# Layer norm shift as a TensorE product, own buffers for the modulation products, partition moves on GpSimd: one change to a two-layer encoder trunk

## Chip, core and metric

The kernel runs on one core of one Trainium2 chip. A core has TensorE (PE; PEld is its weight load), VectorE (DVE), ScalarE (ACT), GpSimd (POOL) and SyncE (SP, which here only issues DMAs). The metric is the device time of one execution in microseconds. Times before are a median of three runs; one more execution was profiled.

## The reference

Two layers on x of 512 tokens by 1024 features, float32. Layer 0 mixes tokens by windowed attention (8 query heads, 2 key/value heads, a sink per head), layer 1 by a recurrent block (a convolution of width 4 and a gated linear recurrence in both directions). A squared-ReLU MLP with 4096 hidden features follows each. Each of the four sub-layers is modulated by the condition `c` and ends in a layer norm:

```python
for i in range(DEPTH):                     # 2 layers, two sub-layers each
    shift, scale, gate = split(silu(c) @ ada_w[i, 0] + ada_b[i, 0], 3)
    h = x * (1.0 + scale) + shift
    y = windowed_gqa(h, ...) if i % 2 == 0 else recurrent_block(h, ...)
    x = layer_norm(ALPHA * x + (1.0 + gate) * y, ln_g[i, 0], ln_b[i, 0])
    shift, scale, gate = split(silu(c) @ ada_w[i, 1] + ada_b[i, 1], 3)
    y = square(relu((x * (1.0 + scale) + shift) @ mlp_w1[i])) @ mlp_w2[i]
    x = layer_norm(ALPHA * x + (1.0 + gate) * y, ln_g[i, 1], ln_b[i, 1])
```

So the norm of one sub-layer and the modulation of the next are one affine step: with n the normalised x, h = n · g(1 + scale) + (b(1 + scale) + shift).

## The kernel before

**Instructions and order.** Python code adds operations to a list with a priority (`Program.add`), a planner (`schedule`) gives each a modelled cost, simulates the five engines and emits them in the order of the simulated starts. So a changed cost, buffer or priority changes the order on every engine. Each engine, and each DMA queue (SP's, POOL's), works in that order. All instructions are emitted at one line, 483; the profile's groups are told apart by tile names.

**Products.** A float32 matrix is split into a rounded high part and a remainder, and a product is three TensorE passes (`mm3`). Weights come in units of 128 x 1024 floats (512 KB): SP loads one into one of four `raw` slots, ScalarE writes the high part into one of six `w` slots, VectorE subtracts for the low part (`conv_unit`). `keep_raw` holds slots back from the weights. Activations lie transposed in `ht` (8192 columns: high, then low), hidden ones in `hid`.

**Modulation.** A row of 1024 (a shift, scale or gate) is a gemv, `gemv_tasks`: eight 512 KB pieces of `ada_w` are loaded, each into a `raw` slot, and VectorE multiplies each by a column of silu(c) and adds into an accumulator. Then the partitions are summed, by TensorE with a matrix of ones in the attention part and by GpSimd's all-reduce in the first MLP. The tasks wait in a list; `bg` takes some after each head (`BH`), each value tile (`BV`) or each tile group of the MLP (`RATE`). Rows for later are kept in DRAM (`mods`). `mod_rows` folds norm and modulation: `rows[3]` becomes g(1 + scale) and `rows[4]` the shift b(1 + scale) + shift, each on all 128 partitions.

**Layer norm.** `last_sink` evacuates an output tile of 128 tokens (`evac`: gate, residual add, statistics) and `ln_block` finishes it. For each half of 512 features ScalarE normalises, VectorE multiplies by `rows[3]` into `u` and adds `rows[4]` into `h`, TensorE transposes `h` in four 128 x 128 blocks into a PSUM bank, and ScalarE and VectorE split the bank into `ht`. The next products need it. Three norms do this, four tiles of two halves each; the last norm writes the output instead. Then VectorE and an accumulating DMA of GpSimd (`xb<-rows`) make the residual.

**Moves between partitions.** Partial rotary embedding (`rope`) packs 32 rows of up to four heads, rotates them together and moves them back (10 moves). In the recurrent block 128-wide tiles hold blocks of 96 channels and a third of a fourth block: `conv` moves 32 rows of the high and low part (6 per group of tiles, four groups), `gates` moves 9 sigmoid outputs and 4 collected tiles per group. All 86 are DMAs on SP's queue. GpSimd's queue has 9 accumulating DMAs of the recurrence (`w<-w`, `ex<-ex`) and 12 of the norms.

Of the kernel before, what the change touches and what calls it, by code (L numbers as in the profile page):

```python
# [14 lines left out]
D = 1024  # L15
# [55 lines left out]
def pack(inp):  # L71
# [91 lines left out]
    out["ident"] = np.eye(128, dtype=np.float32)  # L163
    return out
# [13 lines left out]
class View:  # L178
# [20 lines left out]

    def partition_broadcast(self, n):  # L200
        return View(self.tile, self.p0, self.p1, self.cols, self.ops + (("pb", n),))
# [11 lines left out]
    def get(self):  # L213
        v = self.tile.real[:, :]
        for op in self.ops:
            if op[0] == "i":
                v = v[op[1]]
            elif op[0] == "r":
                v = v.rearrange(op[1], **op[2])
            elif op[0] == "pb":  # L220
# [13 lines left out]
class Program:  # L234
# [60 lines left out]
    def price(self, op, reads, writes):  # L295
        n = 1
        w = writes[0] if writes else reads[0]
        for d in w.shape[1:]:
            n *= d
        op.table, op.nbytes = 0, 0  # L300
        ps = any(v.tile.kind == "ps" for v in reads)
        aps = sum(isinstance(op.kw.get(k), View) for k in ("scalar1", "scalar2", "scalar", "bias", "scale", "accum_out"))
        if op.eng == "tensor":
            passes = 1 if op.fn == "transpose" or op.kw["rhs"].ops[-1][0] == "b" else 4
            op.nbytes = passes * n * (reads[0].p1 - reads[0].p0) / 128
            op.cost = 109 if op.fn == "transpose" else max(107 if passes == 1 else 213, passes * n * 0.4167 + 16)
        elif op.eng == "scalar":
            op.cost = n * 0.833 + (51 if ps else 94) + 93 * aps
            op.table = TABLES.get(op.kw["func"].name, 0) if "func" in op.kw else 0
        elif op.eng == "vector":  # L310
            if op.fn == "bn_stats":
                op.cost = reads[0].shape[1] * 1.042 + 68
            elif op.fn in ("tensor_scalar", "tensor_copy") and not ps:
                op.cost = n * 0.52 + 69 + 60 * aps
            elif op.fn == "tensor_tensor_scan":
                op.cost = n * 2.083 + 65
            else:
                op.cost = n * 1.042 + 65 + (60 if aps else 0)
        elif op.eng == "gpsimd" and op.fn == "dma_start":
            op.cost = 1000  # L320
        elif op.eng == "gpsimd":
            op.cost = {"memset": n * 0.85, "tensor_scalar": n * 3.4 + 105, "partition_all_reduce": n * 7.0}.get(op.fn, n * 2.105 + 147)
        else:
            p = w.shape[0]
            op.nbytes = p * n * 4
            op.cost = 600
        op.end = op.start = None

        n_in = sum(v.tile.kind == "sb" and v.shape[-1] > 0 for k, v in op.kw.items() if isinstance(v, View) and k in ("in0", "in1", "in_", "data0", "data1"))
        if op.eng == "vector":  # L330
            two = n_in == 2 or op.fn in ("tensor_scalar", "tensor_copy") and not ps and writes[0].tile.kind == "sb" and n % 2 == 0
            op.lock = two
        else:
            op.lock = op.eng == "gpsimd" and op.fn not in ("memset", "dma_start")

    def schedule(self):
# [36 lines left out]
        while len(order) < total:  # L373
# [101 lines left out]
    def emit(self, nc, tc, pools):  # L475
        fix = lambda a: self.real(a, pools)
        with tc.manual_schedule():
            order = self.schedule()
            self.place(order, pools)
            for op in order:  # L480
                args = [fix(a) for a in op.args]
                kw = {k: fix(a) for k, a in op.kw.items()}
                op.ins = getattr(getattr(nc, op.eng), op.fn)(*args, **kw)  # L483
# [3 lines left out]
        [128, "ht", "rows", "acc2"]  # L487
        + [f"ex{i}" for i in range(17) if i not in (12, 13)]
# [5 lines left out]
        + [f"hid{i}" for i in range(16)]  # L494
# [36 lines left out]
class Kernel:  # L531
    def __init__(self, I, O):
# [6 lines left out]
        self.ht = t("ht", 8192)  # L539
        self.hid = [t(f"hid{i}", 512) for i in range(16)]  # L540
        self.xb = [t(f"xb{i}", 1024) for i in range(TB)]
        self.rx = t("rows", 6144)
        self.rows = [self.rx[:, 1024 * i : 1024 * i + 1024] for i in range(5)]
        self.ex = [t(f"ex{i}", 512) if i not in (12, 13) else self.rx[:, 512 * i - 1024 : 512 * i - 512] for i in range(17)]
        self.ident = t("ident", 128)
# [12 lines left out]


    def renew(self, kind, idx):  # L560
        n = {"hid": 512, "xb": 1024, "ex": 512, "w": 2048}[kind]
        for i in idx:
            getattr(self, kind)[i] = self.region(f"{kind}{i}", n)
# [87 lines left out]
    def HT(self, k, lo=0, hi=512):  # L651
        a = k * 512
        return self.ht[:, a + lo : a + hi].bitcast(F32R), self.ht[:, 4096 + a + lo : 4096 + a + hi].bitcast(F32R)
# [5 lines left out]
    def fill(self):  # L659
# [16 lines left out]
        BH=3,  # L676
        QE='aavavavava',
        PE='ava',
        BO=(-100, 0, 100),
# [5 lines left out]
        AP0='vvvvvvvv',  # L685
# [16 lines left out]
        XV=(1, 1, 1),  # L702
    )
# [27 lines left out]
    def gemv_tasks(self, idx, part, acc, dst, sink_row=None, red=None, ap="vvvvvvvv"):  # L731
# [4 lines left out]
        def load(k):  # L736
            def f():
                if k < KT:
                    assert self.free_r
                    r = self.free_r.pop(0)  # L740
                    state[k] = r
                    nc.sync.dma_start(
                        out=self.raw[r][:, :], in_=self.I["adaw"][idx, k * 128 : (k + 1) * 128, part * D : (part + 1) * D]
                    )
# [3 lines left out]
                if k > 0:  # L748
                    r = state.pop(k - 1)
                    raw, c = self.raw[r][:, :], self.sc[:, k - 1 : k]  # L750
                    how = ap[k - 1]
                    if how != "v":
# [7 lines left out]
                    self.free_r.append(r)  # L760
# [26 lines left out]
    def mod_rows(self, shift, tmp):  # L787

        v = self.nc.vector
        r = self.rows  # L790
        v.scalar_tensor_tensor(out=tmp, in0=r[3][:, :], scalar=1.0, in1=r[2][:, :], op0=ALU.add, op1=ALU.mult)
        v.tensor_tensor(out=r[4][:, :], in0=shift, in1=tmp, op=ALU.add)
        v.scalar_tensor_tensor(out=r[3][:, :], in0=r[3][:, :], scalar=1.0, in1=r[1][:, :], op0=ALU.add, op1=ALU.mult)
        for i in (1, 2):
            self.nc.scalar.activation(out=r[i][:, :], in_=r[i][:, :], func=AF.Copy, scale=ALPHA)
# [23 lines left out]
    def ln_block(self, t, last=False, parts=1):  # L819
# [18 lines left out]
        for fh in range(2):  # L838
# [28 lines left out]
            hv = self.ht[:, a : a + 2048].rearrange("p (k n) -> p k n", k=4)[:, :, t * 128 : t * 128 + 128]  # L867
            lv = self.ht[:, 4096 + a : 4096 + a + 2048].rearrange("p (k n) -> p k n", k=4)[:, :, t * 128 : t * 128 + 128]
# [93 lines left out]
    def setup(self):  # L962
# [12 lines left out]
        self.mods = [Tile_("dr", f"mods{i}", 1024) for i in range(4)]  # L975
# [21 lines left out]
    def rope(self, heads, how):  # L997
# [16 lines left out]
        for i, (p, dst) in enumerate(heads):  # L1014
            nc.sync.dma_start(out=dst[0:32, :], in_=self.rows[4][32 * i : 32 * i + 32, 0:512])

    def attn(self):
# [7 lines left out]
        def OT(h, lo=0, hi=512):  # L1025
# [3 lines left out]
            a = (i - 4) * 1024  # L1029
            return self.ht[:, a + lo : a + hi].bitcast(F32R), self.ht[:, a + 512 + lo : a + 512 + hi].bitcast(F32R)  # L1030
# [88 lines left out]
        self.renew("ex", range(10))  # L1119
        self.keep_raw = 2  # L1120
# [29 lines left out]
        for n in range(2):  # L1150
# [6 lines left out]
            late.append((p, Q(6 + n, 0, 512)))  # L1157
        self.rope(late, self.P["QE"][8:])
# [85 lines left out]
        for h in order:  # L1244
# [7 lines left out]
        self.renew("ex", range(10))  # L1252
        self.renew("hid", range(8, 16))
        self.flush_bg()
        self.modes = self.P["OM"]
        self.mod_rows(accv, r[4])
# [45 lines left out]
    def load_mods(self, gate, shift, scale, ln, tmp):  # L1302
# [4 lines left out]
        if scale is not None:  # L1307
            nc.sync.dma_start(out=self.rows[3][:, :], in_=self.mods[scale][0:1, :].partition_broadcast(128))
            nc.sync.dma_start(out=self.rows[4][:, :], in_=self.mods[shift][0:1, :].partition_broadcast(128))
            self.mod_rows(self.rows[4][:, :], tmp)  # L1310
# [27 lines left out]
    def rnn(self, nsplit):  # L1338
# [6 lines left out]
        self.renew("ex", range(3, 9))  # L1345
        self.renew("hid", range(14, 16))
        xr = [self.hid[14][:, :], self.hid[15][:, :], ex[16][:, :]]
        XC = [ex[j] for j in range(3)]
        XCH = [ex[3 + j] for j in range(3)]
        XCL = [ex[6 + j] for j in range(3)]  # L1350
        GEL = [ex[9 + j] for j in range(3)]
# [25 lines left out]
        def conv(g):  # L1377
            for j in range(3):
# [9 lines left out]
                for dst, src in ((DH, XCH), (DL, XCL)):  # L1388
                    nc.sync.dma_start(out=dst[32 * j : 32 * j + 32, :], in_=src[j][96:128, :])

        def gates(g):

            u0 = at["g", g]
            for half, blocks in enumerate(GATE_BLOCKS):
                u = u0 + half
                self.prep(u, ahead=2)
                for i, j in enumerate(blocks):
                    xh, xl = (DH, DL) if j == 3 else (XCH[j][:, :], XCL[j][:, :])
                    x = xh[:BW, :].bitcast(F32R), xl[:BW, :].bitcast(F32R)
                    for t in range(3):  # L1400
# [6 lines left out]
                        if j < 3:  # L1407
                            nc.sync.dma_start(out=RI[3, j][32 * t : 32 * t + 32, :], in_=dst[96:128, :])
                    if j < 3:
                        nc.sync.dma_start(  # L1410
                            out=self.rx[96:128, j * 1536 : j * 1536 + 1536], in_=self.w[NW - 1][32 * j : 32 * j + 32, 0:1536]
                        )
                    else:
                        nc.sync.dma_start(out=self.rx[96:128, 4608:6144], in_=self.w[NW - 1][96:128, 0:1536])
# [63 lines left out]
        self.load_mods(0, 1, 2, 2, self.acc2)  # L1478
# [3 lines left out]
        self.renew("ex", range(3, 9))  # L1482
# [6 lines left out]
    def build(self, stop=99):  # L1489
# [3 lines left out]
        if stop == 1:  # L1493
            return self.dump()
        accs, red = (self.acc2, self.rows[1][:, :]), self.ex[8:10]
        gemvs = [(1, 2, self.rows[0], None), (2, 1, self.rows[3], None), (2, 0, self.rows[4], None)]
# [4 lines left out]
        self.bgq.append(lambda: self.mod_rows(self.rows[4][:, :], self.acc2))  # L1501
        self.bgq.append(self.rnn_cols)
        self.keep_raw, self.bg_rate = 2, self.P["RATE"]
# [12 lines left out]
        self.load_mods(3, None, None, 3, self.acc2)  # L1516
# [33 lines left out]
```

## Time and profile before

| | us |
|---|---|
| runs | 1191.2, 1193.58, 1193.3 (median 1193.3) |
| profiled execution, its own time | 1195.24 |
| its span, first to last instruction | 1193.3 |

Stages by the profile's time: input and first projections 0 to 80 us, heads, value and output projection with the first norm to about 206, first MLP with the second norm to about 580, recurrent block with the third norm to 842, second MLP to 1177, last norm to the end. The profile gives busy times per engine and stage, what each instruction waited for, and the clock that TensorE was granted. Matmuls are pipelined, so the mean of one (370 ns) is longer than their distance.

### The profile page before, as it was taken

To read this page: it belongs to the slowest core of one execution; us is meant where nothing else is said; L and a number is where in the kernel's file an instruction comes from. 1 tells how busy PE (TensorE), PEld (TensorE's weight loads), DVE (VectorE), ACT (ScalarE), POOL (GpSimd) and SP (SyncE) were. 2 spreads that over 40 slices of the span, in tenths; PEclk is the share of its full clock that TensorE was granted. 3 is DMA by queue.
4 is the path that set the end of the run, shared out by engine and by line. 5 is a ranking of instruction groups with operands and counts; after the bars stand their busy time and mean duration, and the time that the engine had idled before them with its cause. 6 is when DMAs were issued, how large, how long until landed. Compare 5 with 4: busy or idle time off the path is not lost.

```text
span 1193.3 us, 14277 instructions
## 1 busy us (share of the span) xinstructions
PE 1137.3 (95%) x5268; PEld 929.6 (78%) x5268; DVE 838.3 (70%) x1253; ACT 523.7 (44%) x774; POOL 95.7 (8%) x66
## 2 busy tenths in 40 slices
PE   6989998999999999999999998979999999999995
PEld 4877667988788878887887876868888888888885
DVE  8876979878878975449848888699744444444447
ACT  5455645512321342324368989824522322322411
POOL 1000000122222220000000000000100000000004
PEclk9999998999999999999999998989999999999998
DMA  9752663767677654222534574543732222222201
GB/s 348 287 188 76 212 246 106 196 210 247 200 246 244 247 195 154 100 95 55 151 106 121 139 181 111 151 142 125 211 106 89 99 95 91 104 88 106 89 1 71
DMA packets 56683, 179.99 MB, mean 151 GB/s; under 512 B 7891, under 2 KB 8403, under 8 KB 56614
## 3 DMA queue, kind: packets, MB, share of 16 engines
q1 hardware_dynamic: 53590, 170.44, 42.1%
q0 software_dynamic: 3024, 8.65, 4.0%
q8 instruction: 41, 0.67, 0.2%
q14 instruction: 28, 0.23, 0.1%
HBM read 160.56 MB, written 2.11 MB: 136 GB/s over the span
## 4 chain that ended last, share of the span: by engine, by line
PE 60%; DVE 16%; DMA 8%; ACT 8%; issue 4%; POOL 2%; SPq 1%; DVEq 0%; ACTq 0%; POOLq 0%
PE ps L483 60%; DVE ex L483 4%; DVE w L483 3%; DMA raw<-in_adaw 3%; DVE rows L483 3%; ACT w L483 2%; ACT rows L483 2%; POOL ex L483 2%; DVE xb L483 2%; DVE acc L483 2%; DMA rows<-w 1%; ACT L483 1%; DMA rows<-rows 1%; DVE st L483 1%; ACT ex L483 1%
## 5 line engine op out<-in xcount | busy, mean ns | idle before, releaser
L483 PE MATMUL ps<-ht,w 128*128 128x512 f32 (+1 forms) x2664 | 557.7, 370 | 3.1 <-ACT ht L483 1.8
L483 PEld LDWEIGHTS ps<-ht,w 128*128 128x128 f32 x2664 | 461.4, 190 | 90.1 <-ACT ht L483 2.7
L483 PE MATMUL ps<-w,hid 128*128 128x512 f32 (+1 forms) x1800 | 414.3, 390 | 2.2 <-ACT w L483 1.4
L483 DVE TENSOR_TENSOR w<-raw,w 128x1024 fp32r<-128x1024 f32 x192 | 237.2, 1240 | 226.7 <-ACT w L483 226.4
L483 PEld LDWEIGHTS ps<-w,hid 128*128 128x128 f32 x1800 | 334.1, 188 | 75.6 <-ACT w L483 1.8
L483 ACT CAST w<-raw 128x1024 fp32r<-128x1024 f32 x192 | 198.4, 1040 | 409.6 <-PE ps L483 304.8
L483 PE MATMUL ps<-w,ht 128*128 128x512 f32 (+1 forms) x336 | 75.5, 376 | 6.3 <-DVE w L483 5.2
L483 PEld LDWEIGHTS ps<-w,ht 128*128 128x128 f32 x336 | 57.5, 193 | 19.3 <-DVE w L483 5.6
L483 DVE SCALAR_TENSOR_TENSOR acc<-raw,sc,acc 128x1024 f32<-128x1024 f32 x40 | 55.4, 1385 | 17.1 <-DMA raw<-in_adaw 17.0
L483 DVE SCALAR_TENSOR_TENSOR ex<-rows,ps 128x512 f32<-128x512 f32 (+1 forms) x81 | 53.0, 671 | 19.7 <-PE ps L483 19.7
L483 DVE SCALAR_TENSOR_TENSOR rows<-raw,sc,rows 128x1024 f32<-128x1024 f32 x40 | 55.7, 1394 | 14.3 <-DMA raw<-in_adaw 14.1
L483 ACT ACTIVATE rows<-ps 128x512 f32<-128x512 f32 x66 | 39.1, 593 | 55.8 <-PE ps L483 55.7
L483 DVE TENSOR_TENSOR xb<-xb,ex 128x512 f32<-128x512 f32 (+1 forms) x81 | 55.8, 701 | 1.1 <-ACT xb L483 0.5
L483 DVE TENSOR_TENSOR hid<-ex,hid 128x512 fp32r<-128x512 f32 x66 | 45.5, 690 | 6.4 <-ACT hid L483 1.3
L483 DVE TENSOR_TENSOR ex<-rows 128x512 f32<-128x512 f32 x64 | 47.4, 742 | 1.6 <-ACT rows L483 1.5
L483 ACT ACTIVATE hid<-rows 128x512 fp32r<-128x512 f32 x64 | 40.5, 633 | 1.9
L483 ACT ACT_TABLE_LOAD x26 | 33.4, 1283 | 3.2 <-DMA w<-w 2.0
L483 PE MATMUL ps<-ident,ex 128*128 128x128 f32 x124 | 21.7, 294 | 13.6 <-DVE ex L483 13.5
L483 POOL TENSOR_TENSOR ex<-xb,rows 128x512 f32<-128x512 f32 x5 | 6.8, 1378 | 328.7 <-ACT xb L483 328.7
L483 POOL DMA_DIRECT2D xb<-rows x12 | 11.0, 919 | 262.3 <-DVE mv L483 136.3
L483 DVE TENSOR_TENSOR rows<-rows,ex 128x512 f32<-128x512 f32 x32 | 20.6, 683 | 15.4 <-DMA rows<-rows 12.4
L483 ACT ACTIVATE xb<-xb,mv 128x512 f32<-128x512 f32 x29 | 22.3, 810 | 19.9 <-DVE mv L483 19.8
(142 smaller groups left out, 803.8 us busy)
## 6 DMA issues: line engine op xcount, KB each, us to landing
raw<-in_W SPq DMA_DIRECT2D x184, 512.0 KB
raw<-in_adaw SPq DMA_DIRECT2D x80, 512.0 KB
ex<-in_ada0t SPq DMA_DIRECT2D x28, 256.0 KB
xb<-rows POOLq DMA_DIRECT2D x12, 512.0 KB, 5.9
rows<-w SPq DMA_DIRECT2D x16, 192.0 KB
raw<-in_W SPq DMA_DIRECT2D x8, 288.0 KB
rows<-rows SPq DMA_DIRECT2D x36, 64.0 KB
xb<-in_xT SPq DMA_DIRECT2D x8, 256.0 KB
```

The source lines that it names most:

```text
L483: op.ins = getattr(getattr(nc, op.eng), op.fn)(*args, **kw)
```

## The change

The shift is no longer added by VectorE. `mod_rows` builds, from four DRAM quarters on four partitions, a 36 x 256 matrix `ex[8]` (high part on partitions 0 to 3, remainder on 32 to 35) and a 36 x 512 selector `ex[9]`; the transposes then accumulate into one bank, and a product of the two adds the shift to the transposed tile. Scale and shift rows of the first two norms go through `mods` in DRAM (two more rows).

```diff
-    def mod_rows(self, shift, tmp):
+    def mod_rows(self, ln, shift, scale):
...
-        v.scalar_tensor_tensor(out=tmp, in0=r[3][:, :], scalar=1.0, in1=r[2][:, :], op0=ALU.add, op1=ALU.mult)
-        v.tensor_tensor(out=r[4][:, :], in0=shift, in1=tmp, op=ALU.add)
         v.scalar_tensor_tensor(out=r[3][:, :], in0=r[3][:, :], scalar=1.0, in1=r[1][:, :], op0=ALU.add, op1=ALU.mult)
...
+        self.renew("ex", (8, 9))
+        sel, tmp = r[4][0:36, 0:512], [self.acc2[0:4, i * 256 : i * 256 + 256] for i in range(3)]
+        nc.sync.dma_start(out=sel, in_=self.I["sel"])
+        nc.scalar.copy(out=self.ex[9][0:36, :].bitcast(F32R), in_=sel)
+        nc.sync.dma_start(out=tmp[0], in_=self.I["lnb4"][ln])
+        for i, row in ((1, scale), (2, shift)):
+            nc.sync.dma_start(out=tmp[i].rearrange("p (f c) -> p f c", f=2), in_=self.mods[row][0:1, :].quarters())
+        v.scalar_tensor_tensor(out=tmp[1], in0=tmp[1], scalar=1.0, in1=tmp[0], op0=ALU.add, op1=ALU.mult)
+        v.tensor_tensor(out=tmp[2], in0=tmp[2], in1=tmp[1], op=ALU.add)
+        nc.gpsimd.memset(self.ex[8][0:36, 0:256], 0.0)
+        nc.scalar.copy(out=self.ex[8][0:4, 0:256].bitcast(F32R), in_=tmp[2])
+        v.tensor_tensor(out=self.ex[8][32:36, 0:256].bitcast(F32R), in0=tmp[2], in1=self.ex[8][0:4, 0:256], op=ALU.subtract)
...
-                (v if self.par("GE") == "v" else nc.gpsimd).tensor_tensor(out=u, in0=xh, in1=self.rows[3][:, c], op=ALU.mult)
-                v.tensor_tensor(out=h, in0=u, in1=self.rows[4][:, c], op=ALU.add)
+                v.tensor_tensor(out=h, in0=xh, in1=self.rows[3][:, c], op=ALU.mult)
...
-                nc.tensor.transpose(pt[:, j * 128 : j * 128 + 128], h[:, j * 128 : j * 128 + 128], self.ident[:, :])
+                nc.tensor.transpose(pt[:, j * 128 : j * 128 + 128], h[:, j * 128 : j * 128 + 128], self.ident[:, :], start=j == 0)
+            bm, sel = self.ex[8][0:36, fh * 128 : fh * 128 + 128].bitcast(F32R), self.ex[9][0:36, :].bitcast(F32R)
+            nc.tensor.matmul(pt[:, :], lhsT=bm, rhs=sel, start=False, stop=True, skip_group_check=True)
```

Gemv pieces go into buffers of their own: two neighbouring `ex` or `hid` tiles make one (`exa`, `exb`, `exc`, `hida`), and from the fourth head (`SW`) the low half of the split `ht` gives four more. `keep_raw` is 0 in the attention part. `BH` goes from 3 to 6 tasks per head, their priority offset (`BO`) from -100 to 0, and `AP0` lets ScalarE scale four of the first gemv's eight pieces, which a DMA of GpSimd then adds to the accumulator.

```diff
-                    r = self.free_r.pop(0)
-                    state[k] = r
...
+                    state[k] = self.own[self.n_big % len(self.own)]
+                    self.n_big += 1
+                    nc.sync.dma_start(out=state[k], in_=self.I["adaw"][idx, k * 128 : (k + 1) * 128, part * D : (part + 1) * D])
...
-                        nc.gpsimd.tensor_tensor(out=acc, in0=raw, in1=acc, op=ALU.add)
+                        nc.gpsimd.dma_start(out=acc, in_=raw, accum_op=ALU.add)
...
-        self.keep_raw = 2
+        self.keep_raw = 0
+        self.own = self.big[:2]
...
-        self.keep_raw, self.bg_rate = 2, self.P["RATE"]
+        self.own = [self.big[i] for i in self.P["OWN"]]
+        self.bg_rate = self.P["RATE"]
```

The 86 moves are issued by GpSimd, and the planner's prices for its DMAs change: 500 instead of 1000 ns for a plain issue, 870 for an accumulating one; landing 1.5 to 5 us behind it by size, instead of 4.

```diff
-            nc.sync.dma_start(out=dst[0:32, :], in_=self.rows[4][32 * i : 32 * i + 32, 0:512])
+            nc.gpsimd.dma_start(out=dst[0:32, :], in_=self.rows[4][32 * i : 32 * i + 32, 0:512])
...
-                    nc.sync.dma_start(out=dst[32 * j : 32 * j + 32, :], in_=src[j][96:128, :])
+                    nc.gpsimd.dma_start(out=dst[32 * j : 32 * j + 32, :], in_=src[j][96:128, :])
...
-                            nc.sync.dma_start(out=RI[3, j][32 * t : 32 * t + 32, :], in_=dst[96:128, :])
+                            nc.gpsimd.dma_start(out=RI[3, j][32 * t : 32 * t + 32, :], in_=dst[96:128, :])
...
-            op.cost = 1000
+            op.nbytes = w.shape[0] * n * 4
+            op.cost = 870 if "accum_op" in op.kw else 500
...
-                    op.end += 4000
+                    if "accum_op" in op.kw:
+                        op.end += 5000 if op.nbytes > 300000 else 2600
+                    else:
+                        op.end += 2700 if op.nbytes > 100000 else 1500
```

The two moves of collected tiles in `gates` change in the same way. Tiles in SBUF are laid out anew for the paired buffers.

More of the change, by code (lines that the diff above doesn't have):

```diff
@@ L163, in pack @@
     out["ident"] = np.eye(128, dtype=np.float32)
+    out["lnb4"] = np.ascontiguousarray(out["lnb"].reshape(4, 2, 4, 128).transpose(0, 2, 1, 3).reshape(4, 4, 256))
+    sel = np.zeros((36, 512), np.float32)
+    for j in range(4):
+        sel[[j, 32 + j], j * 128 : j * 128 + 128] = 1.0
+    out["sel"] = sel
     return out
@@ L493 @@
         + [192]
-        + [f"hid{i}" for i in range(16)]
+        + [f"hid{i}" for i in range(10)]
+        + ["hida"]
+        + [f"hid{i}" for i in range(12, 16)]
     )
@@ L544, in __init__ @@
         self.ex = [t(f"ex{i}", 512) if i not in (12, 13) else self.rx[:, 512 * i - 1024 : 512 * i - 512] for i in range(17)]
+        self.ex[0], self.ex[2] = self.pair("exa")
+        self.ex[4], self.ex[6] = self.pair("exb")
+        self.ex[10:12] = self.pair("exc")
+        self.big = [a[:, :].tile[:, :] for a in (self.ex[10], self.hid[10], self.ex[0], self.ex[4])]
+        self.n_big, self.own = 0, []
         self.ident = t("ident", 128)
@@ L562, in renew, with renew_ht @@
         for i in idx:
-            getattr(self, kind)[i] = self.region(f"{kind}{i}", n)
+            if kind == "hid" and i in (10, 11):
+                self.hid[10:12] = self.pair("hida")
+            else:
+                getattr(self, kind)[i] = self.region(f"{kind}{i}", n)
+    def renew_ht(self):
+        self.ht = [self.region("hth", 4096), self.region("htl", 4096)]
     def small(self, tag, n=4):
@@ L974, in setup @@
         self.st = {}
-        self.mods = [Tile_("dr", f"mods{i}", 1024) for i in range(4)]
+        self.mods = [Tile_("dr", f"mods{i}", 1024) for i in range(6)]
         cT, sg = self.small("cT", 8), self.small("sg", 8)
@@ L1157, in attn @@
             late.append((p, Q(6 + n, 0, 512)))
+        self.renew_ht()
+        own = self.region("htl", 4096)
+        more = self.own + [own[:, i * 1024 : i * 1024 + 1024] for i in range(4)]
         self.rope(late, self.P["QE"][8:])
@@ L1243, in attn @@
         uo = N_WQ + 4
-        for h in order:
+        for i, h in enumerate(order):
+            if i == self.P["SW"]:
+                self.own = more
             head(h)
@@ L1251, in attn @@
             nc.scalar.activation(out=self.xb[t][:, :], in_=self.xb[t][:, :], func=AF.Copy, scale=ALPHA)
-        self.renew("ex", range(10))
-        self.renew("hid", range(8, 16))
         self.flush_bg()
+        self.renew("hid", [8, 9, 10, 12, 13, 14, 15])
+        self.ht[1] = self.region("htl", 4096)
         self.modes = self.P["OM"]
-        self.mod_rows(accv, r[4])
+        for row, src in ((4, r[3]), (5, accv)):
+            nc.sync.dma_start(out=self.mods[row][0:1, :], in_=src[0:1, :])
+        self.mod_rows(0, 5, 4)
         self.keep_raw = 0
@@ L1308, in load_mods @@
             nc.sync.dma_start(out=self.rows[3][:, :], in_=self.mods[scale][0:1, :].partition_broadcast(128))
-            nc.sync.dma_start(out=self.rows[4][:, :], in_=self.mods[shift][0:1, :].partition_broadcast(128))
-            self.mod_rows(self.rows[4][:, :], tmp)
+            self.mod_rows(ln, shift, scale)
     def rnn_cols(self):
@@ L1494, in build @@
             return self.dump()
+        self.renew("ex", (8, 9))
         accs, red = (self.acc2, self.rows[1][:, :]), self.ex[8:10]
[L1496 removed]
+        gemvs = [(1, 2, self.rows[0], None), (2, 1, self.rows[3], 4), (2, 0, None, 5)]
         gemvs += [(2, 2, None, 0), (3, 0, None, 1), (3, 1, None, 2), (3, 2, None, 3)]
```

72 lines of the change are left out of this document (39 added, 33 removed).

## The prediction

> **What bounds the kernel now.** The page comes first, for the busy shares, the granted clock and the chain.
>
> ```profile
> span 1193.3 us, 14277 instructions
> PE 1137.3 (95%) x5268; PEld 929.6 (78%) x5268; DVE 838.3 (70%) x1253; ACT 523.7 (44%) x774; POOL 95.7 (8%) x66
> PEclk9999998999999999999999998989999999999998
> PE 60%; DVE 16%; DMA 8%; ACT 8%; issue 4%; POOL 2%; SPq 1%; DVEq 0%; ACTq 0%; POOLq 0%
> ```
>
> TensorE is busy for 95%, so only what interrupts it can be won. The view of busy time by stage shows where that is; its columns are the stage, its length, then PE, PEld, DVE, ACT and POOL busy, the granted clock, DMA share and GB/s.
>
> ```profile
> 60.00:80.00 20.00, 16.15 (x111) 14.13 (x110) 15.99 (x22) 10.56 (x17) 0.00 (x0) 0.97 0.61 197
> 112.00:152.00 40.00, 37.86 (x155) 25.87 (x153) 33.51 (x74) 22.48 (x59) 0.95 (x1) 1.00 0.66 213
> 152.00:182.00 30.00, 28.08 (x119) 21.41 (x120) 25.31 (x33) 12.22 (x16) 0.95 (x1) 1.00 0.64 230
> 182.00:196.00 14.00, 8.45 (x40) 6.32 (x38) 14.00 (x39) 9.41 (x14) 0.00 (x0) 0.95 0.33 112
> 196.00:325.00 129.00, 128.45 (x676) 110.60 (x676) 107.79 (x149) 43.30 (x61) 28.12 (x14) 0.98 0.64 202
> 546.00:576.00 30.00, 25.22 (x145) 21.57 (x144) 28.22 (x62) 13.26 (x20) 2.76 (x3) 0.94 0.35 82
> 576.00:605.00 29.00, 29.00 (x161) 25.60 (x162) 17.66 (x24) 11.27 (x17) 0.85 (x1) 0.94 0.48 141
> 650.00:700.00 50.00, 47.70 (x204) 37.69 (x203) 43.53 (x59) 46.85 (x72) 3.44 (x4) 1.00 0.53 137
> 700.00:750.00 50.00, 46.17 (x190) 37.00 (x189) 41.94 (x57) 45.86 (x68) 2.58 (x3) 0.93 0.57 151
> 750.00:795.00 45.00, 38.98 (x165) 30.84 (x164) 35.96 (x45) 27.43 (x39) 0.00 (x0) 0.97 0.48 155
> 795.00:812.00 17.00, 17.00 (x67) 13.50 (x67) 14.65 (x29) 2.39 (x3) 0.00 (x0) 0.89 0.25 94
> 812.00:842.00 30.00, 27.96 (x194) 25.26 (x193) 29.73 (x64) 16.14 (x24) 2.58 (x3) 1.00 0.48 145
> 842.00:1177.00 335.00, 334.99 (x1529) 277.29 (x1528) 160.37 (x210) 101.55 (x130) 6.96 (x6) 1.00 0.28 94
> ```
>
> Length less PE busy is PE's idle time: 3.9 us around the rope, 2.1 and 1.9 us among the heads, 5.6 us in the first layer norm, 4.8 in the second, 2.3, 3.8 and 6.0 us in the recurrent block, 2.0 us in the third norm, 0.6 us in the stage after the first: 33.0 us. Length times one minus the clock is what slow clock costs on top: 0.6, 0.7, 2.6, 1.8, 1.7, 3.5, 1.4 and 1.9 us in these rows, 14.2 us, each time during or just after a stall. So about 47 us can be won at all; the second MLP (842 to 1177) has none, and the tail, whose norm the change leaves alone, isn't touched. The view of waits says whom PE waited for:
>
> ```profile
> PE ps L483 <- DVE ex L483: 13.5, 7, 4.3
> PE ps L483 <- DVE w L483: 6.1, 2, 5.2
> PE ps L483 <- DMA ex<-rows: 3.9, 1, 3.9
> PE ps L483 <- DMA hid<-ex: 1.8, 2, 1.1
> ```
>
> The first is the layer norm: transposes wait for the vector chain that makes `h`. The last two are moves between partitions.
>
> **The change part by part: layer norm.** Its longest stall and the price of the edit stand here: PE's transposes, the group of all the vector adds of the shift, and the price of one TensorE product of 512 columns.
>
> ```profile
> 196.07 1.97 PE L483 MATMUL ps<-ident,ex 128*128 128x128 f32 x8 [4.35 <-DVE ex L483]
> L483 DVE TENSOR_TENSOR ex<-ex,rows 128x512 f32<-128x512 f32 x24 | 15.6, 682 | 0.0
> L483 PE MATMUL ps<-w,hid 128*128 128x512 f32 x744 | 170.9, 391 | 0.0
> ```
>
> An add took 0.68 us. Eight leave each of three norms: 5.5 us of a DVE that is full there (14.00 of 14 us, 28.22 of 30, 29.73 of 30). Four of them stand ahead of PE's last long stall: 2.7 us earlier. In exchange PE gets eight products per norm at 170.9/744 = 0.23 us: 1.8 us, 5.5 us over three norms. One hides where PE would wait anyway, and costs full price elsewhere; each also delays its own eviction by 0.23 us. The product of the before trace has 128 rows, the new one 36; that smaller case isn't shown, so I bound it between zero and 0.23 us and take 0.23, its nearest row.
>
> The modulation rows (`mod_rows`) lose two 1024-wide vector operations and gain three narrow ones; these rows show the old ones where they stand ahead of a weight conversion for which PE waits (third norm).
>
> ```profile
> 788.83 1.22 DVE L483 SCALAR_TENSOR_TENSOR acc<-rows 128x1024 f32<-128x1024 f32 x1
> 790.56 1.22 DVE L483 TENSOR_TENSOR rows<-rows,acc 128x1024 f32<-128x1024 f32 x1
> 792.84 1.22 DVE L483 TENSOR_TENSOR w<-raw,w 128x1024 fp32r<-128x1024 f32 x1
> 794.11 19.66 PE L483 MATMUL ps<-w,ht 128*128 128x512 f32 x74 [5.21 <-DVE w L483]
> L483 DVE TENSOR_SCALAR ex<-ex,rd 128x256 f32<-128x256 f32 x1 | 0.4, 353 | 0.0
> ```
>
> 2.4 us go; three operations of 256 columns at about 0.35 us (last row, the nearest width) come, 1.1 us. ScalarE gets two small copies, POOL a small memset, SP four short loads per call, and in the first norm two stores to DRAM that those loads wait for. They are needed only by the first product behind the transposes; I cost them at nothing, hidden under the out projection, and at up to 3 us where SP's queue holds weight loads behind them. 1.3 us net of DVE are won each time.
>
> First norm: 2.7 us from adds, 1.3 from `mod_rows`, and, as the gemvs end earlier (below), part of the 8.9 us that seven of their products put between 150 and 206:
>
> ```profile
> L483 DVE SCALAR_TENSOR_TENSOR rows<-raw,sc,rows 128x1024 f32<-128x1024 f32 x7 | 8.9, 1279 | 3.1 <-DMA raw<-in_adaw 3.1
> ```
>
> The stall of 5.6 us and its clock loss of 3.3 us (0.7 and 2.6) can't go below the latency of the last tile; I take 5 us off for 1.0 us of products that aren't hidden: **−4.0**. Second norm: 3 us off the 4.8 + 1.8 + 1.7, 1.0 us on: **−2.0**. Third: 1.5 off 2.0, 1.5 on: **0**; its `mod_rows` ahead of the 5.21 us stall: **−1.5**.
>
> **Own buffers for the gemvs.** Products of the modulation take their 512 KB pieces from buffers of their own, so all four `raw` slots serve weights, six tasks follow a head instead of three, and four of the first gemv's eight products go to ScalarE and a DMA that adds. Four times 1.28 us leave DVE in the heads; the cover is ScalarE (22.48 of 40 us busy) and POOL (0.95). That accumulating chain is serial: 5.9 us per 512 KB landing (below), 24 us, within the 80 us of the heads. PE's 2.1 and 1.9 us among the heads shrink: between 0 and 4.0, I take **−2.0**. PE's idle time ahead of the second products of both MLPs, by what ended it, and the last sum over partitions of these gemvs:
>
> ```profile
> L483 PE MATMUL ps<-w,hid 128*128 128x512 f32 (+1 forms) x1800 | 414.3, 390 | 2.2 <-ACT w L483 1.4 <-DVE w L483 0.9
> 173.90 1.88 PE L483 MATMUL ps<-rows,ones 128*128 128x512 f32 x4
> ```
>
> Late weights cost 2.2 us there at most, and four slots instead of two help where gemvs run: **−0.5**.
>
> **Moves by GpSimd.** 86 moves leave SP's queue for POOL's. The nearest rows on POOL are accumulating DMAs of all 128 partitions; the moves are plain, of 32 mostly. Below: the group and landing of such, one burst on SP, then steps of the chain.
>
> ```profile
> L483 POOL DMA_DIRECT2D w<-w x6 | 5.1, 858 | 150.4 <-DVE rows L483 66.4 <-DVE w L483 43.9 <-ACT w L483 37.4
> xb<-rows POOLq DMA_DIRECT2D x12, 512.0 KB, 5.9
> w<-w POOLq DMA_DIRECT2D x6, 256.0 KB, 3.3
> 74.60 2.41 SPq L483 DMA_DIRECT2D ex<-rows  x4
> 700.18 6.23 DMA rows<-rows
> 706.42 5.39 DMA rows<-w
> 731.54 4.40 DMA hid<-ex
> ```
>
> SP issues one move in 2.41/4 = 0.60 us. POOL's plain issue isn't shown: I bound it by 0.3 us, half of SP's, and 0.86, the accumulating one's (the changed planner assumes 0.50), and take 0.7, nearer to the POOL row. A landing of 4.4 to 6.2 us for 64 or 192 KB, against 3.3 us for 256 KB on POOL, says that on SP the move queued with weight loads. On POOL it should land in under 3.3 us: 1 to 3 us earlier per burst, where three bursts reach PE (idle 2.3, 3.8 and part of 6.0 us). Behind a waiting move on POOL stand only other moves and the nine accumulations of the block; on SP, weights no longer stand behind moves. Between +6 and −6; I take **−2.0**. Rope: four issues at 0.7 end 0.4 us later than on SP, so the 3.9 us stall stays: **+0.5**.
>
> The skill speaks against this part. A DMA from GpSimd needs descriptors that GpSimd writes, and the Trainium skill ("SBUF — State Buffer", section "SBUF: two separate sides") says that a vector operation in a two-port mode locks it out until it ends. By that rule moves issued under the convolution would start late. What this trace shows is 858 ns as mean of six issues with DVE 43.53 of 50 us busy, so no lock shows.
>
> **Sum**: −4.0 −2.0 +0 −1.5 −2.0 −0.5 −2.0 +0.5 = −11.5. The profiled execution took 1195.2 us, 1.9 beyond its span: 1183.7. The median of the three shown runs is 1193.3, 1.9 below: **1181.8**.
>
> **Rivals.**
> (A) *Stalls close wholly.* With fewer gaps the clock stays up too, as it did at 1.00 from 842 on. The two norms then give 14 us, the recurrent block 10, heads 3, less 5.5 for products: −22, 1171. For it: DVE is full exactly where PE waits. Against: the rest of each chain (statistics, ScalarE, eviction) stays.
> (B) *Slower: moves late on POOL.* Gates issue a burst of 13 moves per group. At 0.86 us instead of 0.60 the last is 3.4 us later, plus 1 us if the landing is slower too; over four groups 18 us, of which perhaps 12 reach PE with slower clock, and the −2.0 goes: +14, 1196. It decides from about 0.8 us per plain move. For it: the only POOL rows say 0.86, and ACT and DVE are over 40 of 50 us busy there, with little slack. Against: the landings above.
> (C) *The products cost what the adds gave.* If PE waits for latency rather than for DVE's throughput, norms win 2 us and pay 5.5; with −4 elsewhere nothing moves: 1193.
> (D) *The change doesn't do what it says*: gemvs don't finish earlier because the planner, whose costs are changed too, orders otherwise. Heads and first norm then keep 4 us: 1186; within the forecast's range.
> (E) *Moves wait for the vector engine.* In the convolution each of the 24 moves has vector operations of this kind beside it:
>
> ```profile
> L483 DVE TENSOR_SCALAR ex<-hid,rc 128x512 f32<-128x512 f32 x8 | 4.1, 539 | 0.0
> ```
>
> If POOL can't issue until such a one has ended, 24 times 0.54 us, 13 us, come on the block's path: 1195. This is what the skill's rule above would do. Against it stands the even 858 ns.
>
> **Chances.** Forecast with D 0.56 (1174 to 1190), A 0.14 (1163 to 1174), C 0.13 (1190 to 1197), B 0.13 and E 0.04 (1193 to 1207). About 0.2% is what a measurement of this kernel can tell from no change, 2.4 us. Faster by more: 0.56 + 0.14 and a quarter of C, 0.73; within: 0.10, the middle of C with bits of B; slower: 0.17. A range of 1168 to 1198 leaves out half of A and the upper half of B, some 0.15.
>
> **What would show it.** Norms: the wait of PE for DVE `ex` falls from 13.5 us to under 7, and the stages around 190 and 560 show a clock nearer 1.00; if the wait stays, C. Moves: POOL's plain issue by its mean, under or over 0.8 us; PE's wait for DMA `hid<-ex` gone, and landings under 3.3 us; if PE's idle time in the recurrent block grows beyond 12 us, B. Gemvs: the last ones-product of the attention part comes well before 173 us and vector products between 150 and 206 are gone. The forecast is wrong above all if the reordered plan opens a stall that this profile doesn't have, such as a weight conversion behind the denser vector work of the heads.

## The result and the profile after

The changed kernel takes 1208.9 us (median of four executions, 1208.5 to 1209.3), the kernel before beside it 1193.4. The ratio is 1.0131, with a 95% interval of 1.0115 to 1.0146: 1.3% slower, where 1.0% faster was forecast, and outside the range. The profiled execution took 1208.5 us with a span of 1206.8 (before: 1195.2 and 1193.3).

The page of the changed kernel, its span, busy times, granted clock and chain:

```profile
span 1206.8 us, 14385 instructions
PE 1150.5 (95%) x5292; PEld 937.1 (78%) x5292; DVE 820.8 (68%) x1228; ACT 529.9 (44%) x784; POOL 147.5 (12%) x159
PEclk9989999999999999999899988999999999999998
PE 70%; DVE 8%; DMA 7%; issue 7%; ACT 7%; POOL 1%; SPq 0%; DVEq 0%; POOLq 0%; ACTq 0%
```

DVE does 17.5 us less, as the change meant, and its share of the chain falls from 16% to 8%. The share of "issue", which is time in which an engine waits for nothing that the profile names, rises from 4% to 7%. PE is busy 13.2 us longer, for the same products and the 24 new ones.

To see where, I compare stages that hold the same matmul work. The view of busy time by stage, before and then after, with rope, first norm, recurrent block, and block end with third norm (columns as in the prediction: length, then busy times, clock, DMA):

```profile
60.00:90.00 30.00, 26.11 (x151) 21.24 (x150) 22.10 (x49) 17.43 (x40) 0.00 (x0) 0.94 0.55 183
150.00:215.00 65.00, 57.22 (x301) 47.20 (x301) 58.55 (x113) 31.16 (x48) 5.62 (x6) 0.95 0.53 175
650.00:786.00 136.00, 129.33 (x545) 103.23 (x544) 113.38 (x151) 116.35 (x173) 6.01 (x7) 0.97 0.54 148
786.00:862.00 76.00, 68.48 (x416) 59.71 (x415) 66.99 (x116) 34.15 (x47) 3.44 (x4) 0.96 0.52 160
```

```profile
60.40:96.10 35.70, 26.63 (x152) 21.78 (x151) 20.57 (x48) 19.80 (x42) 6.16 (x10) 0.86 0.66 185
160.40:219.90 59.50, 57.53 (x302) 46.04 (x301) 48.78 (x93) 27.02 (x37) 4.66 (x6) 1.00 0.50 153
652.90:800.10 147.20, 134.36 (x546) 107.48 (x545) 116.89 (x155) 118.09 (x175) 32.76 (x60) 0.93 0.51 138
800.10:871.30 71.20, 69.84 (x424) 59.76 (x423) 59.58 (x106) 33.65 (x48) 3.48 (x4) 1.00 0.54 163
```

The first norm is 5.5 us shorter: PE's idle time there (length less PE) falls from 7.8 to 2.0 us and the clock is 1.00 for 0.95. The rope is 5.7 us longer, 5.2 of them idle time of PE, with a clock of 0.86. The recurrent block is 11.2 us longer; 6.2 of them are idle time of PE (12.8 for 6.7), the other 5.0 are the same products run at a lower clock (0.93 for 0.97). Whoever counts only idle time sees little more than half of what the late transfers cost in the block.

PE's waits, the waits of ScalarE for the collected tiles, and the issue time and landing of the moves (views of waits, groups and DMA issues; the first line is from the kernel before, the others are from the changed one):

```profile
ACT w L483 <- DMA rows<-w: 8.1, 5, 2.2
PE ps L502 <- issue: 7.7, 1, 7.7
PE ps L500 <- DVE exb L502: 3.1, 2, 1.7
ACT w L502 <- DMA rows<-w: 19.5, 7, 5.9
L502 POOL DMA_DIRECT2D rows<-rows x36 | 19.4, 590 | 5.6 <-ACT rows L502 4.3 <-issue 0.5
L502 POOL DMA_DIRECT2D hid<-ex x24 | 12.0, 502 | 70.6 <-ACT ex L502 58.4 <-DVE w L502 9.6 <-DVE ex L502 1.7
rows<-w POOLq DMA_DIRECT2D x16, 192.0 KB, 5.3
ex<-rows POOLq DMA_DIRECT2D x4, 64.0 KB, 5.2
```

The norm's wait, PE for DVE, went from 13.5 us to 3.1. In the block GpSimd issues a move in 0.50 to 0.59 us (means of the groups; single ones take up to 0.88), so the issue price is as cheap as hoped. What is dear is the landing: ScalarE's wait for the collected tiles (`rows<-w`) grows from 8.1 to 19.5 us. The 7.7 us for which the profile names nobody are PE's wait ahead of the rope's second batch of moves; PE goes on at 84.59, and by the trace the last of these moves lands at 84.50.

### The profile page after: what moved, and what is told of

It reads as the page before. It is cut to its first block, busy times and chain, and to the rows that moved or that the text cites. A ratio compares the mean times of both kernels' runs of the same rounds, so it can differ in the third digit from the quotient of the medians.

```text
span 1206.8 us, 14385 instructions
## 1 busy us (share of the span) xinstructions
PE 1150.5 (95%) x5292; PEld 937.1 (78%) x5292; DVE 820.8 (68%) x1228; ACT 529.9 (44%) x784; POOL 147.5 (12%) x159
## 4 chain that ended last, share of the span: by engine, by line
PE 70%; DVE 8%; DMA 7%; issue 7%; ACT 7%; POOL 1%; SPq 0%; DVEq 0%; POOLq 0%; ACTq 0%
PE ps L502 69%; DVE w L502 2%; ACT w L502 2%; ACT rows L502 2%; DVE rows L502 2%; DMA rows<-w 1%; DMA rows<-rows 1%; PE ps L500 1%; ACT L502 1%; DVE ex L502 1%; DVE exc L502 1%; POOL rows L502 1%; ACT acc L502 1%; DMA hida<-in_adaw 1%; ACT ex L502 1%
## 5 line engine op out<-in xcount | busy, mean ns | idle before, releaser
L502 PE MATMUL ps<-hth,w 128*128 128x512 f32 (+1 forms) x1776 | 506.8, 370 | 2.5 <-ACT hth L502 1.8
L502 PE MATMUL ps<-w,hid 128*128 128x512 f32 (+1 forms) x1581 | 369.9, 390 | 0.8 <-DVE w L502 0.8
L502 PEld LDWEIGHTS ps<-hth,w 128*128 128x128 f32 x1776 | 322.1, 190 | 60.5 <-ACT hth L502 1.9
L502 PEld LDWEIGHTS ps<-w,hid 128*128 128x128 f32 x1581 | 293.7, 188 | 65.6 <-issue 1.7
L502 PE MATMUL ps<-htl,w 128*128 128x512 f32 (+1 forms) x888 | 325.1, 366 | 0.0
L502 PEld LDWEIGHTS ps<-htl,w 128*128 128x128 f32 x888 | 168.2, 189 | 29.4 <-issue 0.5
L502 PE MATMUL ps<-w,hth 128*128 128x512 f32 (+1 forms) x256 | 67.4, 373 | 3.4 <-ACT hth L502 2.0
L502 PEld LDWEIGHTS ps<-w,hth 128*128 128x128 f32 x256 | 46.2, 191 | 13.4 <-ACT hth L502 2.4
L502 PE MATMUL ps<-w,hida 128*128 128x512 f32 (+1 forms) x219 | 54.0, 388 | 0.0
L502 PEld LDWEIGHTS ps<-w,hida 128*128 128x128 f32 x219 | 40.9, 188 | 8.8
```

## The experiments

The table gives for each stage by how much it is longer (us) than in the kernel before, at equal matmul work: I take the time at which each trace has done the same columns of products, transposes and shift products left out, so that those count as loss where they stand. Stages go by the times of before (rope 60 to 90, heads to 150, first norm to 215, first MLP to 545, second norm to 605, block 650 to 786, its end and third norm to 862). Each row is one execution; two kernels with one order differ by up to 3 us in a stage that no edit touches (after and after_smallw in norm 1), and `prod64`, whose products take as long as those of `after`, differs from it by 4 in norm 3, at a granted clock of 0.95 for 1.00. In the kernels with a new plan the products of the attention part stand in another order. How their loss divides among rope, heads and norm 1 therefore hangs on which products are counted, by 1 to 3.5 us (for `after` 4.7, 6.6 and -6.7 by another choice). The sum of the three and the other columns don't change.

| kernel | to 60 | rope | heads | norm 1 | MLP 1 | norm 2 | block | norm 3 | end | span |
|---|---|---|---|---|---|---|---|---|---|---|
| after | 0.4 | 5.7 | 4.3 | -5.5 | -2.3 | 0.3 | 11.2 | -4.8 | 4.2 | 13.5 |
| moves_sp | 1.5 | 2.1 | 1.3 | -4.7 | -1.6 | -2.6 | -0.1 | -3.8 | 0.7 | -7.2 |
| emit_sp | 0.6 | 5.9 | 5.1 | -0.4 | -2.4 | -1.0 | 4.7 | -1.9 | 0.5 | 11.2 |
| land | 1.4 | 0.2 | 0.9 | -2.9 | -2.3 | 0.4 | 12.0 | -4.4 | 4.3 | 9.6 |
| before_emit_pool | 0.3 | 5.7 | -0.5 | -0.7 | -0.5 | -0.1 | 9.9 | -1.0 | 3.8 | 16.9 |
| after_smallw | 1.1 | 6.1 | 4.1 | -2.3 | -2.2 | -1.1 | -3.8 | -4.8 | 4.1 | 1.2 |
| moves_sp_smallw | 1.1 | 1.3 | 0.9 | -6.3 | 0.0 | 0.4 | -3.1 | -3.8 | 0.7 | -8.8 |
| prod128 | 0.1 | 5.3 | 4.5 | -4.7 | -1.6 | -3.5 | 9.9 | -5.8 | 4.1 | 8.3 |
| best_vvvv | 1.6 | -5.0 | 2.1 | -8.5 | -0.7 | -3.5 | 1.5 | -6.9 | 0.0 | -19.4 |

### Moves back on SP

All 86 moves of the changed kernel go back, and the planner plans anew:

```diff
-            nc.gpsimd.dma_start(out=dst[0:32, :], in_=self.rows[4][32 * i : 32 * i + 32, 0:512])
+            nc.sync.dma_start(out=dst[0:32, :], in_=self.rows[4][32 * i : 32 * i + 32, 0:512])
```

and likewise in `conv` and `gates`.

> Theory (the moves on GpSimd's queue cost more than they save: 6.2 us in the rope, about 11 in the recurrent block, 4.2 at the end): with all 86 moves back on SP and the rest of the change kept, 1187 to 1192 us. PE's wait ahead of the rope's second batch falls from 7.75 us to about 4, and GpSimd is done at the end as soon as SP is. Rival (the new plan of the shift product and of the gemv buffers is at fault): over 1200 us, with the same long waits for rows<-rows in the recurrent block.

1187.9 us, 0.995 of before (0.9933 to 0.9967): theory. PE's wait ahead of the rope's second batch is 4.6 us. The moves carry more than the whole loss; the rest of the change, in the plan made for it, is worth half a per cent.

### Same order, other queue: both ways

`emit_sp` keeps the order of the changed kernel on every engine and issues its moves from SP:

```diff
-                op.ins = getattr(getattr(nc, op.eng), op.fn)(*args, **kw)
+                op.ins = getattr(nc.sync if op.fn == "dma_start" and "accum_op" not in kw else getattr(nc, op.eng), op.fn)(*args, **kw)
```

> The order of every engine is that of the changed kernel; only the 86 moves are issued by SP at the place in the program where GpSimd had them. Theory (landing on GpSimd's queue is late): 1190 to 1196 us, waits for rows<-rows and rows<-w in the block fall by half. Rival (the order itself, planned for landings of 1.5 to 2.7 us, is at fault): 1203 to 1209 us, the waits stay.

1204.0 us, 1.0083 (1.0064 to 1.0102): the rival's time, and the waits mostly stay (16.0 us for `rows<-w`, 19.5 before the edit). The row of the table says why: the block improves from 11.2 to 4.7, but rope and heads keep their loss, though SP issues the moves. So the order is a cause of its own. `before_emit_pool` does the reverse: the order of before, with only the moves issued by GpSimd.

```diff
-                op.ins = getattr(getattr(nc, op.eng), op.fn)(*args, **kw)
+                op.ins = getattr(nc.gpsimd if op.fn == "dma_start" and op.eng == "sync" and isinstance(op.kw["in_"], View) and op.kw["in_"].tile.kind == "sb" and isinstance(op.kw["out"], View) and op.kw["out"].tile.kind == "sb" else getattr(nc, op.eng), op.fn)(*args, **kw)
```

> The kernel before, its order on every engine kept, with its 86 moves issued by GpSimd at the place in the program where SP had them (107 DMAs from GpSimd). Theory (on GpSimd's queue the moves run beside weight loads that SP now issues at once, and land late): the recurrent block loses 5 to 8 us, the rope 1 to 3, and the end 3.7 through a drain of 10.44 us: 1204 to 1210 us. Rival (only the new plan with its prices loses time): the end alone, 1197 to 1200 us.

1213.5 us, 1.0175 (1.0157 to 1.0193), above both expectations: the queue alone costs 5.7 us in the rope, 9.9 in the block and 3.8 at the end. The rope shows the mechanism. Before, SP issued the four moves from 74.60 to 77.01 (the prediction has the row). The timeline goes on, SP first, then PE:

```profile
77.12 1.50 SPq L483 DMA_DIRECT2D raw<-in_W  x3
78.69 4.53 PE L483 MATMUL ps<-hid,ex 128*128 128x256 f32 x10 [3.85 <-DMA ex<-rows]
```

The same place with the moves on GpSimd, timelines of GpSimd, SP and PE:

```profile
77.57 1.97 POOL L483 DMA_DIRECT2D ex<-rows  x4 [9.52 <-issue]
78.26 2.60 SPq L483 DMA_DIRECT2D raw<-in_W  x3
83.84 5.41 PE L483 MATMUL ps<-hid,ex 128*128 128x256 f32 x10 [8.10 <-DMA ex<-rows]
```

On SP the weight loads stand behind the moves and come when the fourth has been issued; PE goes on 4.09 us after the first issue. On GpSimd the loads start 0.69 us after the first move, beside the others, and PE goes on 6.27 us after the first issue. The rest of the delay is that this batch is issued 2.97 us later, since the batch before it landed late too.

The block shows the same at the last 192 KB move of a burst. Before, then with the moves on GpSimd (SP, GpSimd, and the landing of that one move):

```profile
703.68 6.03 SPq L483 DMA_DIRECT2D rows<-w  x4
709.76 1.77 SPq L483 DMA_DIRECT2D raw<-in_W  x3
```

```profile
705.54 8.87 SPq L483 DMA_DIRECT2D raw<-in_W  x5
714.21 0.49 POOL L483 DMA_DIRECT2D rows<-w  x1 [1.79 <-PE ps L483]
rows<-w POOLq DMA_DIRECT2D x1, 192.0 KB, 7.4
```

On SP this move was issued at 709.2, ahead of the three loads, and landed after 3.1 us; on GpSimd five loads are issued around it and it takes 7.4. One burst later it is 3.1 and 6.5 us. By the issue and landing times of both traces these two moves put the block back by 3 to 4 us each; most of the block's others land hardly later (median of the 36 `rows<-rows` moves of the program 2.6 us on SP, 3.0 on GpSimd, from issue to the semaphore's last increment). SP's order had worked as a right of way for the moves. The Trainium skill states the rule ("DMA: Bandwidth & Descriptors", section "Issuing engines are not separate DMA queues"): DMAs of all issuing engines run on the same 16 DMA engines and interleave, and a second issuer saves only the time of issuing. These runs agree as to the sharing: beside the loads the same move lands after 7.4 us for 3.1. The prediction weighed another rule.

### Is it the weight loads?

If moves are late because loads run beside them, small loads must cure them on GpSimd. In the changed kernel and in the one with all moves on SP, each weight load of the recurrent block brings 32 columns (the rest of those weights is left out); the order of each is kept.

```diff
+                if op.idx in self.small:
+                    kw = {k: a[:, 0:32] for k, a in kw.items()}
```

> The changed kernel in its order, but each weight load of the recurrent block brings 32 columns in place of 768 or 1024 (the rest of those weights is left out, so the output isn't the reference's). Theory (moves are late because weight loads share the DMA engines with them): the moves of the block land in 1.8 to 2.7 us instead of up to 7.5, and the block's loss against the kernel with small weights and moves on SP falls from 11 us to under 3. Rival (GpSimd's queue is slow by itself or the order is at fault): landings over 3 us, the loss stays over 7.

> The control of the run above: all moves on SP, weight loads of the block cut to 32 columns (the rest left out). Theory: in this kernel the moves wait little for weights already, so it gains at most 4 us over the 1187.9 us with whole weights. Rival (weight loads delay moves on SP as much): gains 8 us or more.

With moves on GpSimd 1193.9 us (1.0004, 0.9989 to 1.0019), with moves on SP 1183.4 (0.9913, 0.988 to 0.9947). In the block the two now stand at -3.8 and -3.1: GpSimd's loss against SP went from 11.3 us to -0.7, nothing within the scatter. The block's landings in the changed kernel, then with small loads:

```profile
rows<-w POOLq DMA_DIRECT2D x12, 192.0 KB, 5.8
rows<-rows POOLq DMA_DIRECT2D x27, 64.0 KB, 4.2
hid<-ex POOLq DMA_DIRECT2D x12, 64.0 KB, 2.7
```

```profile
rows<-w POOLq DMA_DIRECT2D x12, 192.0 KB, 3.6
rows<-rows POOLq DMA_DIRECT2D x27, 64.0 KB, 2.4
hid<-ex POOLq DMA_DIRECT2D x12, 64.0 KB, 1.8
```

With no load beside it a convolution's move (`hid<-ex`) lands in 1.8 us on GpSimd; it is not a slow queue. The expected bounds were missed in two places: the 192 KB moves stay at 3.6 (2.7 expected), and the kernel with moves on SP gains 4.5 us (4 expected).

### Honest landings for the planner

```diff
-                        op.end += 2700 if op.nbytes > 100000 else 1500
+                        op.end += 5300 if op.nbytes > 100000 else 3700
```

> The plan reckons with landings as measured (5.3 us for the 192 KB moves, 3.7 us for the others, instead of 2.7 and 1.5); issuing stays on GpSimd. Theory (late landing itself costs, whatever the order): 1205 to 1209 us. Rival (an order that reckoned with too short a landing is at fault): 1195 to 1201 us, waits in the block halved.

1205.1 us, 1.0094 (1.0076 to 1.0111). The total is the theory's, the parts aren't: rope and heads fall from 10.0 us of loss to 1.1, so there the order was at fault, planned for landings of 1.5 us. The block stays at 12.0: there honest landings don't help. Why the planner finds no better order in the block was not tried.

### The block or the rope

`block_sp` puts only the 76 moves of the block back on SP, `before_moves` brings only the third part of the change (moves and planner prices) to the kernel before.

> Only the 76 moves of the recurrent block go back to SP, the 10 of the rope stay on GpSimd (35 DMAs from GpSimd in all instead of 111). Theory: the block is as in the kernel with all moves on SP (its loss of 11 us goes), the rope and the heads keep their loss of about 10 us, and GpSimd's drain at the end takes 1.71 + 35 x 0.0816 = 4.57 us instead of 10.76, so the end loses 4 us less: 1193 to 1198 us. Rival (the block was late because of what went before it, or the drain doesn't go by the number of DMAs): over 1202 us, drain still near 10 us.

> The kernel before with only the third part of the change: the 86 moves on GpSimd and the planner's new prices for them. Theory (the moves alone carry the loss): the recurrent block and the end lose 11 and 4 us, the rope up to 6, so 1206 to 1214 us, 1.010 to 1.017 of before, drain 1.71 + 107 x 0.0816 = 10.4 us. Rival (the moves are late only together with the gemv's accumulations and own buffers): rope and heads as before, 1196 to 1203 us.

`block_sp`: 1194.9 us, 1.0004 (0.9988 to 1.002), the theory's time. Its block loses 0.3 us, rope and heads 8.9. `before_moves`: 1220.6 us, 1.021 (1.0179 to 1.0242), more than expected; stage by stage its rope loses 5.5, the block 10.8, the end 3.7, without any of the new buffers and accumulations; the other 6 us lie in other stages and stay unexplained. So the loss doesn't need the other two parts, which together gain (`moves_sp`).

Both runs also test the end. GpSimd's long DRAIN behind its last operation, read from the trace for each number of DMAs that GpSimd had issued in the whole program:

```
DMAs by GpSimd    DRAIN, us    kernels
21                3.42         before, best_vvvv
25                3.75         moves_sp, emit_sp, moves_sp_prod128
35                4.56         block_sp (4.57 expected)
107               10.44        before_moves (10.4 expected), before_emit_pool
111               10.76        after, land, prod128
```

That is 0.0816 us for each DMA, (10.764 - 3.421)/90, and 1.7 us besides, most of which is the wait for GpSimd's last vector operation (1.6 us). In the changed kernel the drain ends 4.25 us after SP has seen all outputs land, and those 4.2 us are the column "end".

### The shift product

The 36 rows are filled up with zeros to 128 (`sel`, its copy, the memset and both operands), and the planner's prices for them are held, so that the order is unchanged; `prod64` does the same with 64.

```diff
-    sel = np.zeros((36, 512), np.float32)
+    sel = np.zeros((128, 512), np.float32)
-        nc.gpsimd.memset(self.ex[8][0:36, 0:256], 0.0)
+        nc.gpsimd.memset(self.ex[8][:, 0:256], 0.0)
```

> The shift product gets 128 rows (92 of them zeros) in place of 36; the order is unchanged. Theory (a product of 36 rows doesn't overlap its weight load with its neighbours): a product falls from 0.43 to 0.23 us, 24 of them give 4.8 us, 1204 us. Rival (it is the change from transposes to a product, or the accumulation onto them, that costs): stays at 0.43 us each and 1208.9.

> The shift product with 64 rows (28 of them zeros) in the changed kernel's order. Theory (TensorE doesn't load weights ahead between a product of up to half its rows and neighbours of all 128): as with 36 rows, 0.43 us from the product's start to the next, with 0.17 us of idle weight loading ahead of it. Rival (it goes by the count of rows): in between 0.31 and 0.43 us, and about 1206 us.

128 rows: 1203.3 us, 1.0077 (1.0047 to 1.0107), the span 5.2 us shorter. That is the theory's time. 64 rows: 1210.1 us in one execution, as with 36. The timelines of PE and weight loads in the first norm, 36 rows and then 128:

```profile
208.57 0.66 PE L500 MATMUL ps<-ident,exa 128*128 128x128 f32 x4
209.15 0.49 PE L502 MATMUL ps<-ex,ex 36*128 36x512 f32 x1
209.57 0.38 PE L502 MATMUL ps<-hth,w 128*128 128x256 f32 x1
209.15 0.18 PEld L502 LDWEIGHTS ps<-ex,ex 36*128 36x128 f32 x1 [0.17 <-issue]
209.57 0.19 PEld L502 LDWEIGHTS ps<-hth,w 128*128 128x128 f32 x1 [0.24 <-issue]
```

```profile
206.56 0.60 PE L500 MATMUL ps<-ident,exa 128*128 128x128 f32 x4
206.91 0.48 PE L502 MATMUL ps<-ex,ex 128*128 128x512 f32 x1
207.22 0.28 PE L502 MATMUL ps<-hth,w 128*128 128x256 f32 x1
206.88 0.19 PEld L502 LDWEIGHTS ps<-ex,ex 128*128 128x128 f32 x1
```

Read the starts, not the durations. With 36 rows the weight load starts only with its product (209.15), the next one only behind it (209.57): from the transposes to the next product it takes 1.00 us, with 128 rows 0.66. By this distance filling up with zeros saves 0.34 us each, 8 us in 24, of which 5 reach the end. With 64 rows the distance is 1.00 again. The Trainium skill has a rule for it ("TensorEngine Tiling (Array Packing)", section "Key Properties"): a change of tiling mode drains TensorE; that page of the Trainium skill lists modes of 64 and of 128 rows. The runs fit this rule, with 36 and 64 rows on one side and 128 on the other, if a product of few rows counts as such a mode. No run shows that it does: what they show is that weights aren't loaded ahead. The trace's 96-row products behave like 128 (0.23 us from start to start, also where one of 128 rows follows).

### What beats both

Moves on SP and 128-row products together:

> Both at once: all 86 moves on SP and the shift product with 128 rows, in the order of the kernel that had the moves on SP alone. Theory (the 36-row product costs 0.6 us where 0.3 would do, and 24 of them stand on the path): 5 to 6 us below that kernel, ratio to before near 0.990. Rival (with the moves back on SP the products lie in gaps): within 2 us of that kernel, 0.994 to 0.996.

1179.8 us, 0.9886 (0.9858 to 0.9914): theory, and more than expected, 8.1 us below the kernel with the moves on SP. The two gains taken one by one add up to 0.9896, within the interval. The last run also gives the first gemv's sums back to DVE:

```diff
-        AP0='avavavav',
+        AP0='vvvvvvvv',
```

> As the kernel with moves on SP and 128-row products, but the first gemv is summed by DVE alone (no ScalarE scaling and no accumulating DMAs from GpSimd in the heads). Theory (the 512 KB accumulating DMAs slow the rope's moves, which lose 2 us there and 1 us in the heads): 2 to 3 us faster than that kernel. Rival (DVE's time in the heads is what matters, which the accumulations relieve): 2 to 5 us slower.

1176.0 us, 0.9841 (0.9822 to 0.9859), the best of all, 3.8 us below the run above, for 2 to 3 expected. Its page and its rope:

```profile
span 1173.9 us, 14361 instructions
61.60:86.60 25.00, 24.15 (x147) 20.38 (x146) 22.76 (x42) 15.85 (x34) 0.00 (x0) 1.00 0.74 250
```

The rope's idle time is 0.9 us, for 3.9 before; without the four 512 KB accumulations of that gemv its `ex<-rows` moves land after a median of 2.8 us, for 4.6 in the run above (from issue to the semaphore's last increment). The order differs too, so what share each has stays open.

## Why the prediction was wrong

**Moves on POOL should land in under 3.3 us, block -2.0.** This is the step that failed: the block lost 11.2 us, 13 off. The premise read SP's landings of 4.4 to 6.2 us as moves waiting behind weight loads. But these three steps of the chain were among the long ones (the median of the 64 KB moves of the block's gates was 2.6 us on SP), and it overlooked what SP's order also did: hold the loads that come after. On GpSimd the moves met more loads, not fewer, and the last move of a burst landed after 7.4 us for 3.1; `before_emit_pool` shows it with nothing else changed, and the small loads show that the loads are the cause. Issue time, on which the forecast's doubt rested (0.7 us taken, 0.50 to 0.59 measured in the block), was no part of it.

**Rope +0.5.** It counted four issues and left the landing as it was; it lost 5.7, from the late landing and from an order planned for 1.5 us. In the block 5.0 of the 11.2 us are slow clock after the stalls, which neither term held; in the rope 5.2 of 5.7 are idle time.

**Products 0.23 us each, eight per norm.** Mis-sized, and outside the bounds given (0 to 0.23). Four transposes alone take 0.44 us, 0.109 each from start to start; with a 128-row product behind them 0.67, with a 36-row one 1.01 to 1.07 (the delay of what follows counted in). So a product costs 0.23 us with 128 rows, just the price taken, and about 0.6 with 36: over 24 some 14 us of PE for 5.5 reckoned. The nearest row in size was not the nearest in kind. The second norm, +0.3 for -2.0 and -3.5 with 128 rows, fits that, but within the scatter (-2.6 in `moves_sp`, with 36 rows).

**The tail isn't touched.** It isn't in its vector work, but GpSimd's drain adds 4.2 us; the term stood at nothing, and the page of the profile doesn't name the drain.

**First norm -4.0, third norm's `mod_rows` -1.5.** Right in mechanism. The first gave -5.5 (-2.3 and -4.7 in two other executions of the same order). At the end of the block the weight conversion no longer waits behind `mod_rows`; PE's wait for it fell from 5.2 to 1.4 us. The stage gave -4.8 with the third norm's products in it, and -5.8 with 128 rows. -1.5 was too small: PE's idle time there fell from 7.5 to 1.4 us, and the clock rose from 0.96 to 1.00. With 64 rows and a clock of 0.95 the stage gave only -0.6.

**Gemv buffers -2.0 in the heads, -0.5 in the first MLP.** The MLP gave -2.3 (0.0 to -2.4 in the kernels with these buffers). In the heads there is a loss of 4.3 in the changed kernel and 0.9 with honest landings, so it comes with the order; in `best_vvvv` rope and heads together gain 1 to 3 us, by the products counted. The last ones-product of the attention part came 8 us earlier (165.95 for 173.90), but eight products of the gemvs still stand between 150 and 206. This part alone was not tried.

**Rivals.** B had the right place and the wrong price: it put the deciding point at 0.8 us per issue, and the loss came at 0.5. B's sign, over 12 us of idle time in the block, decides nothing, since the prediction's three rows of the block sum to 12.1 before the change. C holds for the size of the products only, since the norm's wait did go. E falls: the 24 moves of the convolution were issued in 0.50 us on average and 0.59 at most, where E needs 0.54 us more for each.

## What to carry to other kernels

Before a small urgent transfer gets a queue of its own, ask what its old queue held back for it: in one queue the order is a right of way, in two everything shares the DMA engines. A planner's landing time must be measured at the place and under the load where it is used. A product of 64 rows or fewer that goes between 128-row ones should be filled up to their rows with zeros, if TensorE is the bound; 96 rows needed no filling here.

## What the hardware showed unexpectedly

- GpSimd's drain at the end of the program takes 0.0816 us for each DMA that it issued, whenever that was: 3.42 us for 21, 10.76 for 111.
- A product of 36 or 64 rows between 128-row ones costs 0.34 us or a little more than one of 128 rows: 0.6 for 0.23. No weights are loaded ahead across it.
- A 64 KB move with no load beside it lands in 1.8 us from GpSimd (`hid<-ex` with small loads); beside loads the groups of such moves have medians of 2.7 to 5.2 us.
